# A two-layer hybrid encoder: the MLP's moving operand laid out in one run, the query norm of one attention group applied inside the exponential, attention weights normalised on VectorE

## The chip, the cores and the metric

The kernel runs on one core of one Trainium2 chip. The metric is the device time of one execution in microseconds. Engines are named as in the profile: PE is TensorE's matrix products (PEld its weight loads), DVE is VectorE, ACT is ScalarE, POOL is GpSimd, SP is SyncE, which here issues most of the DMAs.

## The reference

Two layers act on 256 tokens of width 2048, all in float32. Each layer normalises `x`, projects it once, and feeds three groups of attention heads from that one projection; the group outputs are normalised, concatenated and projected back. Then comes a squared-ReLU MLP of width 8192.

```python
for l in range(DEPTH):
    h = rmsnorm(x, norm_mix[l])
    proj = jnp.einsum('bsd,de->bse', h, w_in[l])
    qa, ka, va, qb, kb, vb, qc, kc, vc = jnp.split(proj, IN_SPLITS, axis=-1)
    oa = window_attention(...)
    ob = neighborhood_attention(...)
    oc = axial_global_attention(...)
    mix = jnp.concatenate([rmsnorm(oa, out_gain_a[l]), rmsnorm(ob, out_gain_b[l]), rmsnorm(oc, out_gain_c[l])], axis=-1)
    x = x + jnp.einsum('bse,ed->bsd', mix, w_o[l])
    h = rmsnorm(x, norm_mlp[l])
    u = jax.nn.relu(jnp.einsum('bsd,df->bsf', h, w_up[l]))
    x = x + jnp.einsum('bsf,fd->bsd', u * u, w_down[l])
return rmsnorm(x, norm_final)
```

The group that the change touches most is C, 16 query heads on 4 key heads of 64 columns:

```python
q = axial_rope(rmsnorm(q, q_gain), ang_row, ang_col)
k = axial_rope(rmsnorm(k, k_gain), ang_row, ang_col)
s = jnp.einsum('bqgrd,bkgd->bgrqk', q_blk, k).astype(jnp.float32) * scale
p = jax.nn.softmax(s, axis=-1).astype(v.dtype)
return jnp.einsum('bgrqk,bkgd->bqgrd', p, v)
```

The norm of a query is one number for each token and head, and the rotation is linear. So that number may be applied to the scores instead of the query.

## The kernel before

**Numbers as high and low parts.** Each operand of a product is split into a part rounded for TensorE (`fp32r`) and the rest. A product is then three products: high by high, high by low, low by high.

**Weights.** All weights are streamed in `steps` of 512 KB, 348 to a layer. `load` fetches a step, `split` makes its high part on ACT (L790) and its low part on DVE (L791, `wlo`), two steps ahead of its use. Input projection, output projection and the MLP's second product go through `mode_b` (L441): the activations are the stationary operand, and the weights' 512 columns move (L448 to L450).

**The MLP's first product** (`up_steps`, L613 and L615) is the other way round: a 128-column block of weights is stationary, and the normalised activations `ht` move. `ht` is a tile of `(2, 2, 256)`: part (high, low), block `kk` of 128 features, 256 tokens. L613 multiplies the high weights by both parts at once, so its 512 moving columns for one `kk` are two runs of 256 with another run between them. L615 multiplies the low weights by the high part only. `hprep` (L178) makes these tiles, for the MLP and for the input projection, which takes its stationary operand out of the same layout.

**Attention.** Work of the attention is cut into units of four (head, query block) pairs, 16 to a layer. A unit has three pieces. `unit_scores` (L317) makes the scores on PE, the negated row maximum on DVE, the exponential on ACT with that maximum as its bias and the row sum as a by-product (L345); then DVE takes the reciprocal of the sum (L353), and POOL multiplies the four blocks of weights by it (L355). `unit_transp` (L357) transposes the weights on PE and splits them (ACT L365, DVE L366). `unit_pv` (L368) multiplies by the values (L376, L383) and adds the two halves on DVE (L391, L396). When a pair of units is done, `mix_prep` (L400) prepares the output projection's operand and sums the squares on POOL (L410 to L419).

**The rotary chain** (`rope`, L278) serves group C's keys and queries. DVE squares and sums the raw rows (L283, L285); POOL takes mean and epsilon (L287), the power -1/2 (L235), multiplies the rows by it (L290) and then does the rotation: per block of 128 tokens a product with the cosine table (L296), four with the sine table (L300), and their sum (L508 for the queries, L495 for the keys). The second table's product is written over the tile of the squares. Queries come in two chunks a layer, `qc0` and `qc1`; they leave the projection through ACT (L503), and PE transposes them after the chain (`q_transposes`, L245).

**What sets the order.** Instructions of an engine run in program order. A hand-written planner, `tick` (L160), runs after each weight step and emits waiting pieces, when what they come after was emitted at least a given delay ago, counted in planned microseconds. The delays stand in one line, L49: `D_T` is from a unit's scores to its transposes, `D_RQ` from a chunk of queries to its transposes. In each layer the input projection's eight chunks run in the order of `IN_CHUNKS`, and the attention pieces are slipped between their steps and those of the output projection.

Of the kernel before, what the change touches and what calls it, by code (L numbers as in the profile page):

```python
# [43 lines left out]
def tile_trunk(ctx: ExitStack, tc: tile.TileContext, x_in, w_in, w_o, w_up, w_down,  # L44
# [4 lines left out]
    D_X, D_S, D_SS, D_T, D_PV, D_QK, D_RQ, D_RK, D_SQ = 6.0, 6.0, 7.0, 18.0, 6.0, 6.0, 24.0, 16.0, 6.0  # L49
# [14 lines left out]
    def big(dt, *shape):  # L64
        return dp.tile([P, *shape], dt, tag="big", bufs=24, name=nm("big"))
# [110 lines left out]


    def hprep(key, gcol, j, hT, ss, done, fin_rs, late=0):  # L178
# [99 lines left out]
    def rope(raw, H, which, l, outs):  # L278
# [8 lines left out]
        nc.gpsimd.tensor_scalar(ms, s, 1.0 / 64, EPS, op0=ALU.mult, op1=ALU.add)  # L287
        r = rsqrt(ms, n)
        rv = raw.rearrange("p t h d -> p (t h) d")
        nc.gpsimd.tensor_mul(rv, rv, r.rearrange("p (a o) -> p a o", o=1).to_broadcast([P, n, 64]))  # L290
        t1 = big(F32, NT, H, 64)
        ct, st = ctab[which, l], stab[which, l]
        t2 = sq.rearrange("p (t h d) -> p t h d", t=NT, h=H)
        for t in range(NT):
# [6 lines left out]
            outs(t, t1[:, t, :, :], t2[:, t, :, :])  # L301

# [14 lines left out]
    def unit_scores(u):  # L317
# [11 lines left out]
        if u.kind == "C":  # L329
            for b in range(2):  # L330
                nc.vector.tensor_reduce(negm[:, 2 * b:2 * b + 2], S[b], axis=AX.X, op=ALU.max, negate=True)
            src = [S[s // 2][:, s % 2, :] for s in range(4)]
# [11 lines left out]
        for s in range(4):  # L344
            nc.scalar.activation(p[:, s, :], src[s], AF.Exp, bias=negm[:, s:s + 1],  # L345
                                 accum_out=sums[:, s:s + 1])
# [7 lines left out]
        for s in range(4):  # L354
            nc.gpsimd.tensor_scalar(p[:, s, :], p[:, s, :], rs[:, s:s + 1], 1.0, op0=ALU.mult, op1=ALU.mult)  # L355
# [98 lines left out]
    def layer_steps(l):  # L454
# [12 lines left out]
        def proj_evac(name, banks):  # L467
# [32 lines left out]
            elif name in ("qc0", "qc1"):  # L500
# [8 lines left out]
                rope(raw, 8, "q", l, outs)  # L509
                i = int(name[2])  # L510
                kh, kl = st["k"]["C"]
                for g in range(2):
                    qT = big(F32R, 4, 256)
                    pq = add(lambda g=g, qT=qT: q_transposes(qs, 2 * g, qT), 0.45, delay=D_RQ)
                    for qb in range(2):
                        queue_unit(g_unit(l, st, "C", 2 * i + g, qb, qT, kh, kl, st["V"]["C"]), pq, st["kC"])
# [23 lines left out]
        for name in IN_CHUNKS:  # L540
# [5 lines left out]
            for k in range(nst):  # L546
# [47 lines left out]
        def up_steps(g):  # L594
            for c in range(2):
                fc = 2 * g + c
                box = {}
                for k in range(8):
# [3 lines left out]
                    def mm(wh, wl, k=k, fc=fc, box=box):  # L602
# [3 lines left out]
                        for kk in range(2):  # L606
                            for fs in range(4):
# [5 lines left out]
                                nc.tensor.matmul(o.rearrange("p (s c) -> p s c", s=2), sh, ht[:, :, kk, :],  # L613
                                                 start=s0, stop=False, skip_group_check=True)
                                nc.tensor.matmul(o[:, 0:256], sl, ht[:, 0, kk, :],  # L615
# [105 lines left out]
    def g_unit(l, st, kind, kv, qb, qT, kh, kl, V, bias=None):  # L721
        u = Unit()
        u.kind, u.l, u.kv, u.qb, u.qT, u.kh, u.kl, u.V = kind, l, kv, qb, qT, kh, kl, V
# [226 lines left out]
```

## Time and profile before

| | us |
|---|---|
| median of 3 runs | 2076.85 (2076.42 to 2078.95) |
| the profiled execution | 2079.79 |
| its span, first to last instruction | 2078.0 |

The profile is that of one execution. It gives, for each engine, when each instruction began and how long it took, and infers from semaphores what a waiting instruction waited for. Starts are counted from the first instruction. In a timeline row stand the start and the duration in us, the engine, the line, the operation, what it writes and reads, and in brackets the idle time of the engine before it with what ended it. In a row of a group stand the busy time in us and the mean ns of one, then the idle time. A row of a window gives the stretch, its length, the busy time and instruction count of PE, PEld, DVE, ACT and POOL, the granted clock of TensorE, the busy share of the DMA engines, and GB/s. The first layer's attention lies between about 70 and 310 us of the span, the second's at about 1100 to 1340; the MLPs fill the rest.

### The profile page before, as it was taken

To read this page: it belongs to the slowest core of one execution; us is meant where nothing else is said; L and a number is where in the kernel's file an instruction comes from. 1 tells how busy PE (TensorE), PEld (TensorE's weight loads), DVE (VectorE), ACT (ScalarE), POOL (GpSimd) and SP (SyncE) were. 2 spreads that over 40 slices of the span, in tenths; PEclk is the share of its full clock that TensorE was granted. 3 is DMA by queue.
4 is the path that set the end of the run, shared out by engine and by line. 5 is a ranking of instruction groups with operands and counts; after the bars stand their busy time and mean duration, and the time that the engine had idled before them with its cause. 6 is when DMAs were issued, how large, how long until landed. Compare 5 with 4: busy or idle time off the path is not lost.

```text
span 2078.0 us, 27361 instructions
## 1 busy us (share of the span) xinstructions
PE 2054.5 (99%) x10396; PEld 1736.4 (84%) x10396; DVE 1359.5 (65%) x1634; ACT 1045.0 (50%) x1536; POOL 274.6 (13%) x298
## 2 busy tenths in 40 slices
PE   8999999999999999999999999999999999999998
PEld 7878788888888888888888787888888888888886
DVE  6878976565565555656668789766565556656565
ACT  6657656444344443444556666555344444434444
POOL 0485420000000000000005843200000000000001
PEclk9999999999999999999999999999999999999999
DMA  8654465566666666666656454556656666665663
GB/s 287 182 156 151 152 192 178 186 192 184 194 189 191 188 188 193 187 189 191 187 179 189 142 159 123 193 173 190 192 187 192 190 186 193 190 191 187 191 212 122
DMA packets 107536, 381.25 MB, mean 183 GB/s; under 512 B 11875, under 2 KB 14691, under 8 KB 107404
## 3 DMA queue, kind: packets, MB, share of 16 engines
q1 hardware_dynamic: 107116, 378.45, 58.1%
q8 instruction: 81, 1.33, 0.3%
q10 hardware_dynamic: 288, 1.05, 0.1%
q14 instruction: 51, 0.42, 0.1%
HBM read 377.34 MB, written 2.11 MB: 183 GB/s over the span
## 4 chain that ended last, share of the span: by engine, by line
PE 93%; DVE 3%; POOL 2%; issue 1%; ACT 0%; DMA 0%; SPq 0%; POOLq 0%; DVEq 0%
PE mm L613 23%; PE mm L449 18%; PE mm L448 18%; PE mm L450 18%; PE mm L615 12%; PE tr L364 1%; PE tr L192 1%; DVE wlo L791 1%; PE mm L323 1%; PE mm L324 1%; DVE big L267 1%; POOL big L300 1%; PE tr L383 0%; POOL big L508 0%; POOL sm L235 0%
## 5 line engine op out<-in xcount | busy, mean ns | idle before, releaser
L791 DVE TENSOR_TENSOR wlo<-wraw,whi 128x1024 fp32r<-128x1024 f32 (+1 forms) x697 | 868.5, 1248 | 655.4 <-ACT whi L790 652.9
L790 ACT CAST whi<-wraw 128x1024 fp32r<-128x1024 f32 (+1 forms) x697 | 731.3, 1051 | 914.4 <-PE mm L450 477.3
L613 PE MATMUL mm<-big,whi 128*128 128x512 f32 x2048 | 724.4, 399 | 0.0
L448 PE MATMUL mm<-whi,big 128*128 128x512 f32 (+1 forms) x1792 | 696.2, 389 | 1.0 <-DVE x L585 1.0
L449 PE MATMUL mm<-wlo,big 128*128 128x512 f32 (+1 forms) x1792 | 693.2, 387 | 0.6 <-DVE wlo L791 0.4
L450 PE MATMUL mm<-whi,big 128*128 128x512 f32 (+1 forms) x1792 | 692.4, 386 | 0.0
L615 PE MATMUL mm<-big,wlo 128*128 128x256 f32 x2048 | 575.1, 281 | 0.0
L613 PEld LDWEIGHTS mm<-big,whi 128*128 128x128 f32 x2048 | 384.8, 188 | 95.8
L450 PEld LDWEIGHTS mm<-whi,big 128*128 128x128 f32 x1792 | 337.2, 188 | 68.6
L448 PEld LDWEIGHTS mm<-whi,big 128*128 128x128 f32 x1792 | 337.5, 189 | 67.5 <-DVE x L585 2.2
L449 PEld LDWEIGHTS mm<-wlo,big 128*128 128x128 f32 x1792 | 337.8, 189 | 66.6 <-DVE wlo L791 2.3
L615 PEld LDWEIGHTS mm<-big,wlo 128*128 128x128 f32 x2048 | 386.8, 189 | 0.5
L235 POOL TENSOR_TENSOR sm<-sm,mhalf 128x2 f32<-128x2 f32 (+3 forms) x16 | 23.7, 1482 | 785.0 <-DVE sm L230 770.9
L355 POOL TENSOR_SCALAR big<-big,sm 128x256 f32<-128x256 f32 x128 | 96.0, 767 | 224.7 <-DVE sm L353 200.0
L691 POOL TENSOR_TENSOR x<-x,big 128x512 f32<-128x512 f32 x6 | 8.6, 1456 | 722.6 <-ACT mid L695 722.6
L650 DVE SCALAR_TENSOR_TENSOR x<-mm,sm,x 128x512 f32<-128x512 f32 x128 | 89.9, 743 | 4.5 <-PE mm L450 4.5
L623 ACT COPY mid<-mm 128x256 f32<-128x256 f32 x128 | 46.6, 373 | 26.7 <-PE mm L615 26.7
L624 DVE TENSOR_TENSOR mid<-mid,mm 128x256 f32<-128x256 f32 x128 | 49.4, 419 | 0.0
L625 DVE SCALAR_TENSOR_TENSOR mid<-mid 128x512 f32<-128x512 f32 x64 | 44.0, 688 | 1.1
L629 DVE TENSOR_TENSOR big<-mid,big 128x512 fp32r<-128x512 f32 x64 | 43.8, 684 | 0.0
L366 DVE TENSOR_TENSOR big<-tr,big 128x512 fp32r<-128x512 f32 x64 | 41.1, 680 | 0.8 <-ACT big L365 0.5
L628 ACT CAST big<-mid 128x512 fp32r<-128x512 f32 x64 | 40.1, 626 | 2.8 <-DVE mid L625 0.2
(116 smaller groups left out, 1004.0 us busy)
## 6 DMA issues: line engine op xcount, KB each, us to landing
wraw<-in_w_up_dram SPq DMA_DIRECT2D x256, 512.0 KB, 3.5
wraw<-in_w_down_dram SPq DMA_DIRECT2D x256, 512.0 KB, 3.5
wraw<-in_w_in_dram SPq DMA_DIRECT2D x120, 512.0 KB, 3.6
wraw<-in_w_o_dram SPq DMA_DIRECT2D x64, 512.0 KB, 4.1
biasB<-in_rpb_dram SPq DMA_DIRECT2D x16, 349.5 KB, 5.6
biasA<-avec SPq DMA_DIRECT2D x4, 768.0 KB, 5.7
x<-in_x_dram SPq DMA_DIRECT2D x3, 512.0 KB, 9.5
big<-in_gfin_dram SPq DMA_DIRECT2D x2, 512.0 KB, 4.7
```

What stands on the lines that cost most here:

```text
L355: nc.gpsimd.tensor_scalar(p[:, s, :], p[:, s, :], rs[:, s:s + 1], 1.0, op0=ALU.mult, op1=ALU.mult)
L448: nc.tensor.matmul(o, a_h, wh[:, i, :], start=first and i == 0, stop=False)
L449: nc.tensor.matmul(o, a_h, wl[:, i, :], start=False, stop=False)
L450: nc.tensor.matmul(o, a_l, wh[:, i, :], start=False, stop=last and i == len(sub) - 1)
L613: nc.tensor.matmul(o.rearrange("p (s c) -> p s c", s=2), sh, ht[:, :, kk, :], start=s0, stop=False, skip_group_check=True)
L615: nc.tensor.matmul(o[:, 0:256], sl, ht[:, 0, kk, :], start=False, stop=s1, skip_group_check=True)
L623: nc.scalar.copy(ai, o[:, 256:512])
L624: nc.vector.tensor_add(ai, ai, o[:, 0:256])
L625: nc.vector.scalar_tensor_tensor(a, a, 0.0, a, op0=ALU.max, op1=ALU.mult)
L650: nc.vector.scalar_tensor_tensor(xs, box["b"][t], st["r2"][:, t:t + 1], xs, op0=ALU.mult, op1=ALU.add)
L790: last_hi[0] = nc.scalar.copy(h[:, part], w[:, part]).ins
L791: nc.vector.tensor_sub(lo[:, part], w[:, part], f(h[:, part]))
```

## The change

There are three edits, and two planned delays that go with them.

1. `hprep` makes its tiles as `(2, 512)`: block `kk`, then both parts side by side, 256 columns each. A helper, `halves`, shows such a tile in the old order of axes to everything else that uses it. In `up_steps` both moving operands are now one run.
2. For the queries of group C, `rope` rotates the raw rows. Mean, epsilon and power are done on POOL behind the rotation and kept in a tile `rq`. The row maximum is multiplied by `rq` on DVE, and the exponential takes `rq` as its scale. The keys keep the old way. The second table's product gets a tile of its own, `t2`.
3. The four products of the weights with the reciprocal of the sum move from POOL to DVE.

`D_T` goes from 18 to 15 and `D_RQ` from 24 to 20.

```diff
-    D_X, D_S, D_SS, D_T, D_PV, D_QK, D_RQ, D_RK, D_SQ = 6.0, 6.0, 7.0, 18.0, 6.0, 6.0, 24.0, 16.0, 6.0
+    D_X, D_S, D_SS, D_T, D_PV, D_QK, D_RQ, D_RK, D_SQ = 6.0, 6.0, 7.0, 15.0, 6.0, 6.0, 20.0, 16.0, 6.0
...
+    def halves(rows):
+
+        return rows.rearrange("p k (s c) -> p s k c", s=2)
...
-            hh = big(F32R, 2, 2, 256)
-            hT[2 * j + h] = hh
+            rows = big(F32R, 2, 512)
+            hT[2 * j + h] = rows
+            hh = halves(rows)
...
-        nc.gpsimd.tensor_scalar(ms, s, 1.0 / 64, EPS, op0=ALU.mult, op1=ALU.add)
-        r = rsqrt(ms, n)
-        rv = raw.rearrange("p t h d -> p (t h) d")
-        nc.gpsimd.tensor_mul(rv, rv, r.rearrange("p (a o) -> p a o", o=1).to_broadcast([P, n, 64]))
+        if which == "k":
+            nc.gpsimd.tensor_scalar(ms, s, 1.0 / 64, EPS, op0=ALU.mult, op1=ALU.add)
+            r = rsqrt(ms, n)
+            rv = raw.rearrange("p t h d -> p (t h) d")
+            nc.gpsimd.tensor_mul(rv, rv, r.rearrange("p (a o) -> p a o", o=1).to_broadcast([P, n, 64]))
         t1 = big(F32, NT, H, 64)
+        t2 = big(F32, NT, H, 64)
         ct, st = ctab[which, l], stab[which, l]
-        t2 = sq.rearrange("p (t h d) -> p t h d", t=NT, h=H)
...
+        if which == "k":
+            return
+        nc.gpsimd.tensor_scalar(ms, s, 1.0 / 64, EPS, op0=ALU.mult, op1=ALU.add)
+        r = sp.tile([P, n], F32, tag="rq", bufs=3, name=nm("rq"))
+        nc.gpsimd.tensor_tensor(r, ms, mhalf[:, 0:n], op=ALU.pow)
+        return r
...
+            nc.vector.tensor_mul(negm, negm, u.rq)
...
             nc.scalar.activation(p[:, s, :], src[s], AF.Exp, bias=negm[:, s:s + 1],
+                                 scale=u.rq[:, s:s + 1] if u.kind == "C" else 1.0,
                                  accum_out=sums[:, s:s + 1])
...
-            nc.gpsimd.tensor_scalar(p[:, s, :], p[:, s, :], rs[:, s:s + 1], 1.0, op0=ALU.mult, op1=ALU.mult)
+            nc.vector.tensor_scalar(p[:, s, :], p[:, s, :], rs[:, s:s + 1], None, op0=ALU.mult)
...
-                    hts = [st["hT"][(k * nk + i) // 2] for i in range(nk)]
+                    hts = [halves(st["hT"][(k * nk + i) // 2]) for i in range(nk)]
...
-                                nc.tensor.matmul(o.rearrange("p (s c) -> p s c", s=2), sh, ht[:, :, kk, :],
-                                                 start=s0, stop=False, skip_group_check=True)
-                                nc.tensor.matmul(o[:, 0:256], sl, ht[:, 0, kk, :],
+                                nc.tensor.matmul(o, sh, ht[:, kk, :], start=s0, stop=False, skip_group_check=True)
+                                nc.tensor.matmul(o[:, 0:256], sl, ht[:, kk, 0:256],
```

**Where instructions move: POOL at the first layer's first chunk of queries.** These are POOL's rows before, from the weights' normalisation (L355) of three units to the end of the queries' rotary chain.

```order
L355 TENSOR_SCALAR big_808<-big_808,sm_824 128x256 x4
L355 TENSOR_SCALAR big_896<-big_896,sm_912 128x256 x4
L355 TENSOR_SCALAR big_1011<-big_1011,sm_1027 128x256 x4
L287 TENSOR_SCALAR sm_1103<-sm_1101 128x16
L235 TENSOR_TENSOR sm_1105<-sm_1103,mhalf 128x16
L290 TENSOR_TENSOR big_1095<-big_1095,sm_1105 128x1024
L296 TENSOR_TENSOR big_1108<-big_1095,ctab_q_443 128x512
L300 TENSOR_TENSOR big_1099<-big_1095,stab_q_444 128x8x16 x4
L296 TENSOR_TENSOR big_1108<-big_1095,ctab_q_443 128x512
L508 TENSOR_TENSOR big_1098<-big_1108,big_1099 128x512
L300 TENSOR_TENSOR big_1099<-big_1095,stab_q_444 128x8x16 x4
L508 TENSOR_TENSOR big_1098<-big_1108,big_1099 128x512
```

And these are POOL's rows at the same place now, where L424 and L429 are the old L410 and L415, L302, L306 and L522 the old L296, L300 and L508, and `rq` is the tile that the exponential's scale comes from.

```order
L424 TENSOR_TENSOR mid_1092<-mid_978 128x512
L429 TENSOR_TENSOR sqacc_1094<-mid_1092 128x256
L302 TENSOR_TENSOR big_1123<-big_1114,ctab_q_443 128x512
L306 TENSOR_TENSOR big_1124<-big_1114,stab_q_444 128x8x16 x4
L302 TENSOR_TENSOR big_1123<-big_1114,ctab_q_443 128x512
L522 TENSOR_TENSOR big_1117<-big_1123,big_1124 128x512
L306 TENSOR_TENSOR big_1124<-big_1114,stab_q_444 128x8x16 x4
L522 TENSOR_TENSOR big_1117<-big_1123,big_1124 128x512
L310 TENSOR_SCALAR sm_1122<-sm_1120 128x16
L312 TENSOR_TENSOR rq_1138<-sm_1122,mhalf 128x16
```

The units' products and the queries' norm stood ahead of the rotation; now the squares of the mix stand there, and mean and power stand behind it. On PE the transposes of these queries stand twelve rows, one weight step, earlier.

**Where instructions move: DVE in the first layer's output projection.** These are DVE's rows before, from the low part of one weight step (`wlo`) on; the lines between belong to units of group B (L342, L353, L396) and to the residual (L585).

```order
L791 TENSOR_TENSOR wlo_2523<-wraw_2286,whi_2522 128x1024
L342 TENSOR_REDUCE sm_2505<-big_2504 128x4
L585 SCALAR_TENSOR_TENSOR x<-mm_2464,sm_1418,x 128x512
L585 SCALAR_TENSOR_TENSOR x<-mm_2465,sm_1418,x 128x512
L791 TENSOR_TENSOR wlo_2543<-wraw_2346,whi_2542 128x1024
L353 RECIPROCAL sm_2514<-sm_2506 128x4
L396 TENSOR_TENSOR mid_2455<-tr_2560,ot_2565 64x2x128 x2
L791 TENSOR_TENSOR wlo_2581<-wraw_2408,whi_2580 128x1024
```

And these are DVE's rows now from the low part of the same weight step on (L807 is the old L791, L355 the old L342, L601 the old L585, L367 the old L353, L443 the old L429, L405 the old L391, L380 the old L366; L369 is the product that came from POOL).

```order
L807 TENSOR_TENSOR wlo_2592<-wraw_2355,whi_2591 128x1024
L355 TENSOR_REDUCE sm_2574<-big_2573 128x4
L601 SCALAR_TENSOR_TENSOR x<-mm_2533,sm_1399,x 128x512
L601 SCALAR_TENSOR_TENSOR x<-mm_2534,sm_1399,x 128x512
L807 TENSOR_TENSOR wlo_2619<-wraw_2407,whi_2618 128x1024
L367 RECIPROCAL sm_2583<-sm_2575 128x4
L443 TENSOR_SCALAR sm_2612<-tr_2609 128x2
L369 TENSOR_SCALAR big_2573<-big_2573,sm_2583 128x256 x4
L405 TENSOR_TENSOR mid_2647<-tr_2636,ot_2645 64x256 x2
L380 TENSOR_TENSOR big_2651<-tr_2652,big_2650 128x512
L380 TENSOR_TENSOR big_2651<-tr_2659,big_2650 128x512
L807 TENSOR_TENSOR wlo_2669<-wraw_2469,whi_2668 128x1024
```

Between two weight splits DVE now has the four products of a unit, and the pieces of the units stand earlier, so that more of them come before a given split. Over the seven weight steps from the low part that before is `wlo_2431` to the one that is `wlo_2702`, there are 16 such products now, and none before.

More of the change, by code (lines that the diff above doesn't have):

```diff
@@ L508, in outs @@
                     nc.gpsimd.tensor_add(qs[:, t, :].rearrange("p (h d) -> p h d", h=8), a, b)
-                rope(raw, 8, "q", l, outs)
+                rq = rope(raw, 8, "q", l, outs)
                 i = int(name[2])
@@ L515, in proj_evac @@
                     for qb in range(2):
-                        queue_unit(g_unit(l, st, "C", 2 * i + g, qb, qT, kh, kl, st["V"]["C"]), pq, st["kC"])
+                        c0 = qb * 8 + 4 * g
+                        queue_unit(g_unit(l, st, "C", 2 * i + g, qb, qT, kh, kl, st["V"]["C"],
+                                          rq=rq[:, c0:c0 + 4]), pq, st["kC"])
             elif name == "qa":
@@ L719, in bias_a, with g_unit @@
         return tb
-    def g_unit(l, st, kind, kv, qb, qT, kh, kl, V, bias=None):
+    def g_unit(l, st, kind, kv, qb, qT, kh, kl, V, bias=None, rq=None):
         u = Unit()
+        u.rq = rq
         u.kind, u.l, u.kv, u.qb, u.qT, u.kh, u.kl, u.V = kind, l, kv, qb, qT, kh, kl, V
```

## The prediction

> **What bounds the kernel now.** I read the page's busy times first, then the chain of work that ended last, then TensorE's (PE's) start times.
>
> ```profile
> PE 2054.5 (99%) x10396; PEld 1736.4 (84%) x10396; DVE 1359.5 (65%) x1634; ACT 1045.0 (50%) x1536; POOL 274.6 (13%) x298
> PE 93%; DVE 3%; POOL 2%; issue 1%; ACT 0%; DMA 0%; SPq 0%; POOLq 0%; DVEq 0%
> L613 PE MATMUL mm<-big,whi 128*128 128x512 f32 x2048 | 724.4, 399 | 0.0
> ```
>
> The chain is 93% PE, so an edit counts if it shortens the step from one matmul to the next, or removes a place where PE stands still. Durations of matmuls overlap (a start every 0.23 us, each 0.39 us long); only start times tell the cost. Three streams of starts:
>
> ```profile
> 549.12 0.39 PE L448 MATMUL mm<-whi,big 128*128 128x512 f32 x1
> ...
> 551.16 0.39 PE L448 MATMUL mm<-whi,big 128*128 128x512 f32 x1
> ...
> 39.82 0.28 PE L450 MATMUL mm<-whi,big 128*128 128x256 f32 x1
> ...
> 41.02 0.28 PE L448 MATMUL mm<-whi,big 128*128 128x256 f32 x1
> ...
> 560.25 0.40 PE L613 MATMUL mm<-big,whi 128*128 128x512 f32 x1
> 560.49 0.28 PE L615 MATMUL mm<-big,wlo 128*128 128x256 f32 x1
> ...
> 561.31 0.40 PE L613 MATMUL mm<-big,whi 128*128 128x512 f32 x1
> ```
>
> Nine 512-column products of one run take 2.04 us, 226.7 ns each. Ten 256-column products take 1.20 us, 120 ns each. The first product of the MLP alternates L613 (512 columns in two runs of 256) with L615 (256): three pairs take 1.06 us, 353.3 ns a pair. The two streams would give 226.7 + 120 = 346.7.
>
> **Edit 1, one run.** The pair costs 6.6 ns more than its two parts do elsewhere, and the only difference I see is the break between the runs. Rounded to the streams' common step (226.7 = 34 x 6.67, 120 = 18 x 6.67, 353.3 = 53 x 6.67) it is one step of 6.67 ns. There are 2048 pairs: 2048 x 6.67 = **13.65 us** saved. Bounds: nothing; and two steps, 27.3 us, for which the first pair after a stream of 512s speaks:
>
> ```profile
> 553.20 0.39 PE L613 MATMUL mm<-big,whi 128*128 128x512 f32 x1
> ...
> 553.54 0.40 PE L613 MATMUL mm<-big,whi 128*128 128x512 f32 x1
> ```
>
> That pair took 0.34 us with its break, once; the next ones take 353. I take one step, since the steady streams give it and 340 is seen only on entering. L613's row has no idle time of PE before it, and the engines that split its weights are busy 65% and 50% of the span, so they can follow a faster PE.
>
> **Edit 2, the norm of C's queries.** The rotary chain on GpSimd (POOL) now ends too late once a layer:
>
> ```profile
> PE tr L245 <- POOL big L508: 5.5, 2, 2.8
> 104.18 3.87 POOL L355 TENSOR_SCALAR big<-big,sm 128x256 f32<-128x256 f32 x4 [10.88 <-DVE sm L353]
> 108.13 1.05 POOL L287 TENSOR_SCALAR sm<-sm 128x16 f32<-128x16 f32 x1
> 109.26 3.76 POOL L235 TENSOR_TENSOR sm<-sm,mhalf 128x16 f32<-128x16 f32 x1
> 113.10 2.15 POOL L290 TENSOR_TENSOR big<-big,sm 128x1024 f32<-128x1024 f32 x1
> 115.33 1.35 POOL L296 TENSOR_TENSOR big<-big,ctab_q 128x512 f32<-128x512 f32 x1
> ...
> 125.77 2.12 POOL L508 TENSOR_TENSOR big<-big,big 128x512 f32<-128x512 f32 x1
> 102.96 1.24 ACT L503 ACTIVATE big<-mm,sm 128x512 f32<-128x512 f32 x2
> 124.89 0.27 PE L245 MATMUL tr<-ident,big 128*128 128x128 f32 x1
> 127.94 0.99 PE L245 MATMUL tr<-ident,big 128*128 128x128 f32 x7 [2.78 <-POOL big L508]
> 128.68 0.48 PE L448 MATMUL mm<-whi,big 128*128 128x512 f32 x1
> ...
> 132.64 0.39 PE L449 MATMUL mm<-wlo,big 128*128 128x512 f32 x1
> 120.00:133.00 13.00, 10.22 (x43) 8.14 (x42) 10.01 (x12) 6.61 (x10) 12.17 (x12) 0.87 0.53 164
> ```
>
> PE's second transpose starts at 127.94 instead of 0.11 after 124.89 (the last seven take 0.74): 2.94 us lost. Then the granted clock is down (0.87 over the window), and ten matmuls from 128.68 to 132.64 take 3.96 us instead of 2.27: 1.69 more. That is 4.63 a layer, **9.3 us** for two.
>
> The raw queries are there at 104.20 (L503's end). POOL is then held by the weights' normalisation (3.87), and by L287, L235 and L290 (to 115.33); all of it leaves the front of the chain. From the first L296 to the last L508 it is 12.56 us. In the changed order, POOL has the mix's L410 and L415 ahead of the chain. They need a VectorE (DVE) result of about the same time, so I start the chain between 104.2 and 108, and it ends between 116.8 and 120.6. PE reaches these transposes twelve rows, one step of 12 x 226.7 = 2.72 us, sooner: 122.2. So there is 1.6 to 5.4 us of room and the wait goes. At the bad end it stays as it is, and nothing is gained.
>
> The mean square and the power stand behind the rope now. Their 1.05 + 3.76 end by 121.6 to 125.4. The new wait is DVE's product of the row maximum with `rq`; DVE's weight splits queue behind it. That unit's scores come only after transposes at 122.2, their copies and a planned delay, so it doesn't bind. It adds 16 products of four columns, 0.26 us each by L351's row (below), in 140 to 200, where DVE is busy 45.81 of 60: free. The scale operand may cost ScalarE up to 32 ns on each of 64 exponentials (a scaled copy, L406, against L345, below), 2 us beside the 41.06 of 60 that it is busy: nothing on PE's path.
>
> **Edit 3, weights normalised on DVE.** 128 pieces leave POOL, which has no time to lose, for an engine that binds in two stretches a layer:
>
> ```profile
> L355 POOL TENSOR_SCALAR big<-big,sm 128x256 f32<-128x256 f32 x128 | 96.0, 767 | 224.7 <-DVE sm L353 200.0 <-DVE sm L429 13.7 <-ACT big L503 10.9
> L707 DVE TENSOR_SCALAR x<-x,sm 128x1024 f32<-128x1024 f32 x2 | 1.5, 754 | 1.3 <-POOL sm L235 1.3
> L353 DVE RECIPROCAL sm<-sm 128x4 f32<-128x4 f32 x32 | 5.5, 172 | 9.8 <-ACT big L345 9.5
> L351 DVE TENSOR_TENSOR sm<-sm,sm 128x4 f32<-128x4 f32 x8 | 2.1, 258 | 3.6 <-ACT sm L350 3.4
> L345 ACT ACTIVATE big<-mm,sm 128x256 f32<-128x256 f32 x64 | 29.5, 472 | 23.3 <-DVE sm L331 22.8
> L406 ACT ACTIVATE big<-mid,gn 128x256 fp32r<-128x256 f32 x32 | 15.0, 504 | 18.5 <-DVE mid L396 6.6 <-POOL big L753 6.5 <-DVE mid L391 3.4
> 92.00:113.00 21.00, 20.70 (x103) 16.96 (x102) 19.52 (x28) 15.38 (x29) 9.95 (x7) 1.00 0.59 173
> 223.28:262.23 38.95, 37.33 (x193) 30.26 (x191) 38.40 (x53) 27.55 (x55) 14.78 (x18) 1.00 0.43 139
> 110.18 0.41 DVE L396 TENSOR_TENSOR mid<-tr,ot 64x256 f32<-64x256 f32 x1
> 110.51 1.27 DVE L366 TENSOR_TENSOR big<-tr,big 128x512 fp32r<-128x512 f32 x2
> 111.24 1.09 PE L383 MATMUL tr<-big,mid 128*128 128x512 f32 x3 [0.30 <-DVE big L366]
> 261.00 1.23 DVE L791 TENSOR_TENSOR wlo<-wraw,whi 128x1024 fp32r<-128x1024 f32 x1
> ...
> 264.75 0.40 PE L449 MATMUL mm<-wlo,big 128*128 128x512 f32 x1
> 140.00:200.00 60.00, 60.00 (x310) 50.99 (x309) 45.81 (x60) 41.06 (x92) 39.04 (x45) 1.00 0.53 166
> ```
>
> The price of a piece is not in the trace. L707 is this very operation with 1024 columns (754 ns), and L353 has 4 (172). On the line between them, 256 columns cost 172 + 252 x 0.571 = 316 ns; I take **0.31 us** as an estimate from those rows. Bounds: 0.172 below, and 0.767 above, what POOL pays (L707's whole duration is about that).
>
> In 92 to 113, DVE is busy 19.52 of 21.00, and PE already waits for L366. Three units bring 12 x 0.31 = 3.7; 1.5 of idle time takes part of it; 2.2 reach PE. In 223 to 262, DVE is busy 38.40 of 38.95. The order puts 16 pieces ahead of the weight split that began at 261.00, and other work that changes places there is worth 0.8 (two more L366, 1.27; two more L353, 0.34; four L396 fewer and two more L391 of that size, -0.82). PE used that split at 264.75, 2.5 after its end. So 16 x 0.31 + 0.8 - 2.5 = 3.3 reach PE. Together 5.5 a layer, **11.0 us** of new stalls; 3.2 with the low price, 36.6 with the high one. The other units fall where DVE has the idle time just shown.
>
> **Sum.** -13.65 - 9.3 + 11.0 = -11.95 us. The profiled execution took 2079.79 us, so 2067.8. That execution lies 2.94 above the median of 2076.85 shown; in terms of the median: **2064.9 us**, -0.58%.
>
> **Rivals.** *The break costs nothing* (the 6.67 ns belongs to alternating long and short products): edits 2 and 3 remain, -9.3 + 11.0, 2078.5. For it: the first pair ran at 0.34 with its break. The Trainium skill (Advanced Engine Details and Errata, SBUF Cachelines) counts the cost of a read by 16-byte lines, and asks for two hits on a line; runs of 256 fp32 fill their lines either way, so by that rule the break is free. Against it: the two steady streams add up to one step less.
>
> *Two steps*: the short product also drops to 113, the pair to 340: 2051.2. For it that same entering pair; against it 120 ns in every steady 256 stream.
>
> *The query wait stays*, because L410's input comes late from a DVE that is now slower in just that stretch: 2074.2.
>
> *DVE becomes the bound*, the case that ends slower. POOL still runs ropes, squares and bias sums in both stretches (9.95 and 14.78 us busy above), and DVE pieces that collide with them take what POOL's did, 0.767: 12 x 0.767 - 1.5 + 16 x 0.767 + 0.8 - 2.5 = 18.3 a layer, 36.6 in all, and 2076.85 - 22.95 + 36.6 = 2090.5. It decides from 28 p - 3.2 = 11.5, a piece of p = 0.52 us.
>
> ```profile
> L355 POOL TENSOR_SCALAR big<-big,sm x128: 470/478/2511, 71.3 to 1303.0; 128x256 f32<-128x256 f32 x128
> ```
>
> The Trainium skill (SBUF — State Buffer, Who interferes with whom) says that a DVE operation in a two-port mode and GpSimd exclude each other for a whole instruction; the spread of POOL's pieces beside a busy DVE (470 to 2511, mean 767) goes that way, but no row has a DVE operation of that kind beside POOL. Against this rival: POOL itself loses 96 us of work, so there is less to collide with.
>
> **Chances.** Forecast 0.53 (its own range 2057 to 2073, from the low price to some of the query wait left), break free 0.12, two steps 0.15, query wait stays 0.07, DVE binds 0.13. A measurement of this kernel can tell about 0.2% from no change, 2072.7 to 2081.0. So faster 0.68 (forecast and two steps), same 0.19 (break free, query wait), slower 0.13. The range takes in all but the last, with the low price beside two steps: 2048 to 2080.
>
> **What would show it.** Edit 1: three pairs of the MLP's first product in 1.04 us (1.06: no gain; 1.02: two steps). Edit 2: PE's row of waits for L508's successor gone, and full clock in 120 to 133. Edit 3: the mean of the new DVE pieces near 310 ns, and PE's waits for L366, L396 and the weight split longer by some 5 us a layer; above 0.52 us a piece I am wrong on the sign.

## The result: slower by 1.2%, and the profile after

| | before | after |
|---|---|---|
| median of 4 runs, us | 2077.86 | 2103.68 (2102.69 to 2104.84) |
| span of the profiled execution, us | 2078.0 | 2102.6 |
| mean granted clock of TensorE | 0.998 | 0.992 |

The ratio is 1.0124, 95% interval 1.0111 to 1.0137. The forecast of 2064.9 has the wrong sign. Line numbers have moved: L613 and L615 are now L629 and L630; L448 to L450 are L462 to L464; L791 is L807; the scaling by the reciprocal, L355, is L369; the exponential L345 is L358; the weights' transposes L364 are L378 and their low half L366 is L380; the product with V, L383, is L397; L396 is L410, L407 is L421, L283 and L285 are L288 and L290, the queries' transposes L245 are L250.

First rows of the page after: busy times, the chain that ended last, and two groups (busy us and mean ns, then idle time before them); the third group is from the view by lines.

```profile
PE 2062.0 (98%) x10396; PEld 1742.7 (83%) x10396; DVE 1398.3 (67%) x1778; ACT 1049.4 (50%) x1536; POOL 176.6 (8%) x166
PE 88%; DVE 9%; issue 1%; ACT 1%; DMA 0%; SPq 0%; DVEq 0%; POOLq 0%; POOL 0%; ACTq 0%
L629 PE MATMUL mm<-big,whi 128*128 128x512 f32 x2048 | 724.4, 399 | 0.0
L369 DVE TENSOR_SCALAR big<-big,sm 128x256 f32<-128x256 f32 x128 | 48.4, 440 | 0.8
L250 PE MATMUL tr<-ident,big 128*128 128x128 f32 x64 | 8.9, 274 | 0.0
```

DVE's share of the chain went from 3% to 9%, while its busy time rose by only 39 us. The MLP's long product has the same 724.4 us as before. The queries' transposes (last row) wait for nothing now. In their place stand other waits; these are PE's, grouped by what it waited for (us in total, times, longest):

```profile
PE tr L397 <- DVE big L380: 15.4, 4, 5.6
PE tr L378 <- ACT big L358: 3.7, 2, 1.9
...
PE mm L463 <- DVE wlo L807: 2.4, 6, 0.7
```

The longest is at the first layer's third unit, and again in the second layer. PE's rows there, then DVE's, then POOL's (start, duration, in brackets idle time and what ended it):

```profile
98.36 1.07 PE L397 MATMUL tr<-big,mid 128*128 128x512 f32 x4
...
101.99 1.03 PE L378 MATMUL tr<-ident,big 128*128 128x128 f32 x8
...
111.04 0.39 PE L397 MATMUL tr<-big,mid 128*128 128x512 f32 x1
117.00 1.65 PE L397 MATMUL tr<-big,mid 128*128 128x512 f32 x3 [5.57 <-DVE big L380]
```

```profile
102.18 0.68 DVE L272 TENSOR_TENSOR big<-tr,big 64x512 fp32r<-64x512 f32 x1
...
103.08 1.40 DVE L272 TENSOR_TENSOR big<-tr,big 64x512 fp32r<-64x512 f32 x2
104.52 0.42 DVE L410 TENSOR_TENSOR mid<-tr,ot 64x256 f32<-64x256 f32 x1
...
105.57 1.20 DVE L807 TENSOR_TENSOR wlo<-wraw,whi 128x1024 fp32r<-128x1024 f32 x1
106.68 3.73 DVE L369 TENSOR_SCALAR big<-big,sm 128x256 f32<-128x256 f32 x4
110.34 1.28 DVE L421 SCALAR_TENSOR_TENSOR big<-mid,gn,big 128x256 fp32r<-128x256 f32 x2
111.55 1.47 DVE L288 TENSOR_TENSOR big<-big 128x1024 f32<-128x1024 f32 x1
112.94 2.28 DVE L807 TENSOR_TENSOR wlo<-wraw,whi 128x1024 fp32r<-128x1024 f32 x1
115.14 1.21 DVE L290 TENSOR_REDUCE sm<-big 128x16 f32<-128x1024 f32 x1
116.27 1.27 DVE L380 TENSOR_TENSOR big<-tr,big 128x512 fp32r<-128x512 f32 x2
```

```profile
105.59 2.07 POOL L424 TENSOR_TENSOR mid<-mid 128x512 f32<-128x512 f32 x1 [17.78 <-DVE mid L410]
...
108.44 1.34 POOL L302 TENSOR_TENSOR big<-big,ctab_q 128x512 f32<-128x512 f32 x1
109.75 2.19 POOL L306 TENSOR_TENSOR big<-big,stab_q 128x128 f32<-128x128 f32 x4
```

PE transposed this unit's weights at 101.99, and DVE wrote their low half only at 116.27. DVE was not idle: it was that far behind, with the next unit's four scalings (3.73 us), the other units' mix (L410, L421), the last of the keys' low parts (L272), the query chunk's squares and sums (L288, L290) and two weight splits (L807) ahead of the low half. PE reached the product with V at 111.04, and stood 5.6 us. The next view, of windows (length, busy us and count of PE, PEld, DVE, ACT, POOL, granted clock, DMA share, GB/s), shows what that cost besides:

```profile
101.90:117.50 15.60, 10.03 (x48) 8.14 (x47) 15.40 (x23) 9.29 (x19) 11.83 (x12) 0.90 0.38 111
114.38:121.21 6.83, 4.21 (x14) 3.62 (x15) 6.79 (x9) 1.75 (x3) 6.75 (x6) 0.50 0.45 130
120.00:133.00 13.00, 13.00 (x61) 10.86 (x60) 8.00 (x12) 5.33 (x8) 5.15 (x4) 0.95 0.65 206
```

DVE is busy 15.40 of 15.60 us while PE is busy 10.03; from 114.38 on the clock is at half for 6.83 us, and its end, at 121.21, is what takes the last row below full clock. In the first of these windows DVE was as full before, and PE hardly idle:

```profile
101.90:117.50 15.60, 15.30 (x75) 12.30 (x75) 15.27 (x19) 11.57 (x20) 13.00 (x10) 1.00 0.71 222
```

So a full DVE does not by itself stop PE; what differs is what stands ahead of the low half when PE asks for it. Lost PE time can be counted as follows: for every matmul, take the step to the next one less the median step of its line and shape, and add up what lies over 20 ns. This gives 54.9 us after and 30.8 before. The 24.1 between them account for nearly all of the 24.6 by which the span grew.

### The profile page after: what moved, and what is told of

It is laid out like the page before. It is cut to its first block, busy times and chain, and to the rows that moved or that the text cites. A ratio compares the mean times of both kernels' runs of the same rounds, so it can differ in the third digit from the quotient of the medians.

```text
span 2102.6 us, 27351 instructions
## 1 busy us (share of the span) xinstructions
PE 2062.0 (98%) x10396; PEld 1742.7 (83%) x10396; DVE 1398.3 (67%) x1778; ACT 1049.4 (50%) x1536; POOL 176.6 (8%) x166
## 4 chain that ended last, share of the span: by engine, by line
PE 88%; DVE 9%; issue 1%; ACT 1%; DMA 0%; SPq 0%; DVEq 0%; POOLq 0%; POOL 0%; ACTq 0%
PE mm L629 23%; PE mm L463 17%; PE mm L464 17%; PE mm L462 17%; PE mm L630 12%; DVE wlo L807 2%; DVE big L369 1%; DVE big L380 1%; ACT big L358 1%; DVE big L272 1%; PE tr L378 1%; PE tr L196 1%; DVE big L421 1%; PE tr L397 1%; DVE big L348 1%
## 5 line engine op out<-in xcount | busy, mean ns | idle before, releaser
L807 DVE TENSOR_TENSOR wlo<-wraw,whi 128x1024 fp32r<-128x1024 f32 (+1 forms) x697 | 862.3, 1239 | 642.5 <-ACT whi L806 640.3
L629 PE MATMUL mm<-big,whi 128*128 128x512 f32 x2048 | 724.4, 399 | 0.0
L462 PE MATMUL mm<-whi,big 128*128 128x512 f32 (+1 forms) x1792 | 697.6, 391 | 4.0 <-DVE big L257 1.7
L464 PE MATMUL mm<-whi,big 128*128 128x512 f32 (+1 forms) x1792 | 694.1, 387 | 0.0
L630 PE MATMUL mm<-big,wlo 128*128 128x256 f32 x2048 | 576.1, 281 | 0.0
L629 PEld LDWEIGHTS mm<-big,whi 128*128 128x128 f32 x2048 | 385.4, 188 | 95.0
L462 PEld LDWEIGHTS mm<-whi,big 128*128 128x128 f32 x1792 | 338.4, 189 | 71.3 <-issue 2.5
L464 PEld LDWEIGHTS mm<-whi,big 128*128 128x128 f32 x1792 | 338.5, 189 | 68.4
L630 PEld LDWEIGHTS mm<-big,wlo 128*128 128x128 f32 x2048 | 387.8, 189 | 0.5
L240 POOL TENSOR_TENSOR sm<-sm,mhalf 128x2 f32<-128x2 f32 (+2 forms) x12 | 12.8, 1067 | 812.9 <-DVE sm L235 782.4
L358 ACT ACTIVATE big<-mm,sm,rq 128x256 f32<-128x256 f32 x64 | 35.3, 561 | 31.2 <-DVE sm L344 31.1
L369 DVE TENSOR_SCALAR big<-big,sm 128x256 f32<-128x256 f32 x128 | 48.4, 440 | 0.8
L424 POOL TENSOR_TENSOR mid<-mid 128x512 f32<-128x512 f32 x16 | 27.1, 1692 | 255.8 <-DVE mid L410 197.1
```

What stands on the lines that cost most here:

```text
L369: nc.vector.tensor_scalar(p[:, s, :], p[:, s, :], rs[:, s:s + 1], None, op0=ALU.mult)
L462: nc.tensor.matmul(o, a_h, wh[:, i, :], start=first and i == 0, stop=False)
L464: nc.tensor.matmul(o, a_l, wh[:, i, :], start=False, stop=last and i == len(sub) - 1)
L629: nc.tensor.matmul(o, sh, ht[:, kk, :], start=s0, stop=False, skip_group_check=True)
L630: nc.tensor.matmul(o[:, 0:256], sl, ht[:, kk, 0:256], start=False, stop=s1, skip_group_check=True)
L807: nc.vector.tensor_sub(lo[:, part], w[:, part], f(h[:, part]))
```

## The experiments

All are timed beside the kernel before, whose medians lay at 2077.05 to 2077.83 in the four sets.

### The edits one at a time

**One run** (edit 1 alone): the kernel before, with `rows = big(F32R, 2, 512)` and both moving operands in one run.

> The kernel before with edit 1 alone (the MLP's moving operand in one run). Theory A (the break between two runs of 256 columns is free): the pair of L613 and L615 stays at 353.3 ns, as in the changed kernel's profile, and the time within 0.1% of before. Theory B (the break costs 6.67 ns, hidden in the changed kernel by something else): 346.7 ns a pair and 13.65 us less.

2078.97 us, ratio 1.0005 (0.9996 to 1.0015). A long and a short product still take 353.3 ns together. The saving of 13.65 us is excluded; in this stream the break between the runs is free. In the changed kernel too, three pairs last 575.50 - 574.43 = 1.07 us:

```profile
574.43 0.40 PE L629 MATMUL mm<-big,whi 128*128 128x512 f32 x1
574.67 0.28 PE L630 MATMUL mm<-big,wlo 128*128 128x256 f32 x1
...
575.50 0.40 PE L629 MATMUL mm<-big,whi 128*128 128x512 f32 x1
```

**Norm in the exponential** (edit 2 alone, with its delay):

```diff
-D_T, ..., D_RQ = 18.0, ..., 24.0
+D_T, ..., D_RQ = 18.0, ..., 20.0
```

> The kernel before with edit 2 alone (norm of C's queries inside the exponential, D_RQ 20; POOL still normalises the weights, D_T 18). If the loss comes from DVE's new pieces alone: the wait of the queries' transposes goes, no half-clock spell behind it, about 9 us less than before. If rotating first also costs (the mix's squares ahead of the chain, the wait for rq): no gain, or up to 5 us more than before.

2072.69 us, ratio 0.9975 (0.9965 to 0.9984): 4.8 us faster. The window that had a granted clock of 0.87 before has full clock:

```profile
120.00:133.00 13.00, 12.90 (x67) 10.57 (x66) 12.24 (x14) 8.63 (x13) 12.18 (x9) 1.00 0.55 165
PE mm L458 <- DVE wlo L803: 3.4, 4, 1.0
```

The wait is gone, and with PE earlier others appear: the second row (of PE's waits) is the weight split, for which PE waited 0.4 us in all before. The gain is about half of the 9 us expected; the part on the prediction comes back to it.

**Weights on DVE** (edit 3 alone, with `D_T` 15; the query norm stays on POOL with `D_RQ` 24):

> The kernel before with edit 3 alone (weights normalised on DVE, D_T 15). If DVE's new pieces are the loss: the queries' wait stays (9 us, in before as well), and new stalls of about 30 us come, so 2100 to 2110. If the loss needs edits 2 and 3 together (POOL's rope begins earlier and meets DVE's pieces): under 2090.

2102.19 us, ratio 1.0118 (1.0103 to 1.0133), so edit 3 with its delay is enough for the whole loss. The places are others than in the whole change: the waits of the queries' transposes for POOL grow from 5.5 to 10.6 us, and the product with V waits 4.9, not 15.4.

**Grouped**: the kernel before, with the MLP's first product in another order, four long products ahead of four short ones; still two runs.

```diff
+for low in range(2):
     for fs in range(4):
...
```

> The kernel before with the MLP's first product in another order: four high products of a feature block, then the four low ones, instead of one high and one low by turns; the same products, the operand still in two runs. If alternating long and short products costs the 6.67 ns: eight products take 4 x 226.7 + 4 x 120 = 1386.8 ns instead of 1413.2, and 2048 pairs 13.5 us less. If the two runs cost them: 1413 ns, no change. If a short product after a short one is what costs 120 (113 after a long one): longer, up to 1440 ns and 13.6 us more.

2072.86 us, ratio 0.998 (0.9971 to 0.9989). In the timeline (x4: four products in one row) four pairs take 593.74 - 592.34 = 1.40 us; the mean is 350.8 ns a pair, and long follows long in 233.6.

```profile
592.34 1.09 PE L611 MATMUL mm<-big,whi 128*128 128x512 f32 x4
593.27 0.64 PE L614 MATMUL mm<-big,wlo 128*128 128x256 f32 x4
593.74 1.09 PE L611 MATMUL mm<-big,whi 128*128 128x512 f32 x4
```

### Edit 3 taken apart: the pieces, their form, the delay

At this point the theory was the pieces themselves: they run beside POOL. By the trace after, 88 of the 128 hardly touch a POOL instruction and take 348 ns on average; the other 40 lie beside POOL, most of them wholly, and take 643 on average (the 667 in an expectation below is not borne out); the longest takes 1380. The rival was the delay of the weights' transposes, which edit 3 cut from 18 to 15.

**After, on POOL**: the changed kernel with one line undone, delay 15.

```diff
-            nc.vector.tensor_scalar(p[:, s, :], p[:, s, :], rs[:, s:s + 1], None, op0=ALU.mult)
+            nc.gpsimd.tensor_scalar(p[:, s, :], p[:, s, :], rs[:, s:s + 1], 1.0, op0=ALU.mult, op1=ALU.mult)
```

> The first two edits with the shorter delay of the weights' transposes (D_T 15), the weights normalised on GpSimd as before. If the 128 pieces on VectorE make the changed kernel slow, this one stays near the run of the second edit alone, 2072.7 us (2069 to 2077), and PE's waits at the product with V shrink to under 1 us each. If the shorter delay does it (PE reaches the weights three rows sooner, before they are normalised), it stays above 2085.

2082.26 us, ratio 1.0022 (1.0013 to 1.0032), between the two. The second edit gave 2072.69 with a delay of 18 (and two runs in the MLP, which by the first run makes no difference); 15 costs 9.6 us with no piece on DVE.

**Pieces out**: the changed kernel without L368 and L369, delay 15; it leaves out the normalisation of the weights.

> The changed kernel without the 128 pieces; it leaves out the normalisation of the attention weights. If the pieces are the whole cost of the third edit: 2068 to 2075 us, and the wait of 5.7 us at the product with V is gone. If a third or more of the cost lies elsewhere (the delay of 15, the order on VectorE): 2080 or more, with waits of over 2 us at the product with V left.

2082.38 us, ratio 1.0022 (1.0013 to 1.0032). Even with no normalisation anywhere the delay's cost is there, and its largest waits are again at the product with V (L395 here):

```profile
PE tr L395 <- DVE big L378: 8.9, 4, 2.3
```

**One product a unit**: the same scaling as one DVE instruction over 1024 columns.

```diff
-        for s in range(4):
-            nc.vector.tensor_scalar(p[:, s, :], p[:, s, :], rs[:, s:s + 1], None, op0=ALU.mult)
+        nc.vector.tensor_tensor(p, p, rs.rearrange("p (a o) -> p a o", o=1).to_broadcast([P, 4, 256]), op=ALU.mult)
```

> The changed kernel with one VectorE product per unit (128 x 1024, the reciprocals spread over the columns) in place of four scalings with a scalar per row. If the cost is the collision of that form of scaling with GpSimd (348 ns a piece alone, 667 beside GpSimd, 1380 at most), the product takes about the same 1.1 to 1.5 us whether GpSimd works or not, the four-piece group of 3.73 us at 106.7 becomes 1.5 or less, and the time falls to 2078 to 2092 us. If it is the plain load on VectorE's queue (1.1 to 1.4 us a unit in either form), the time stays within 5 us of 2103.7.

2103.18 us, ratio 1.0112 (1.0094 to 1.0130): the same as with four pieces, though a unit now costs DVE 1424 ns instead of 4 x 440, and none took over 2064 where a group of pieces took 3.73 us.

```profile
L368 DVE TENSOR_TENSOR big<-big,sm x32: 1206/1226/2064, 71.0 to 1318.2; 128x1024 f32<-128x1024 f32 x32
```

The waits lie elsewhere (the weight split 8.4 us, POOL's sum of squares 6.9, the product with V only 4.3) and come to the same. The collision with POOL is seen in both forms (18 of the products stay clear of POOL and take 1223 ns, 14 lie beside it and take 1682), but its extent doesn't set the time.

**The changed kernel with a delay of 18**: one number differs.

```diff
-D_T = 15.0
+D_T = 18.0
```

> The changed kernel with the weights' transposes delayed by 18 as before, not 15. With GpSimd normalising, 15 for 18 cost 2082.3 - 2072.7 = 9.6 us. If the delay and the pieces cost separately, this gives 2103.7 - 9.6 = 2094 (2091 to 2097), so the pieces cost 21 at either delay. If the pieces hurt only because the delay was cut under them, it comes near 2075 to 2085. If VectorE is full in these stretches whatever the delay, it stays above 2099.

2079.92 us, ratio 1.0010 (1.0001 to 1.0020): 23.8 us come back with one planned number. The expectation that the two costs add (2094) was wrong; it is the case in which the delay was cut under the pieces. The same stretch, PE's rows, then DVE's, then the window:

```profile
102.78 1.03 PE L378 MATMUL tr<-ident,big 128*128 128x128 f32 x8
...
106.39 1.07 PE L397 MATMUL tr<-big,mid 128*128 128x512 f32 x4
...
110.01 1.07 PE L397 MATMUL tr<-big,mid 128*128 128x512 f32 x4
```

```profile
92.53 2.80 DVE L272 TENSOR_TENSOR big<-tr,big 64x512 fp32r<-64x512 f32 x4 [0.70 <-ACT big L270]
...
103.48 2.22 DVE L288 TENSOR_TENSOR big<-big 128x1024 f32<-128x1024 f32 x1
105.63 1.97 DVE L369 TENSOR_SCALAR big<-big,sm 128x256 f32<-128x256 f32 x4
107.52 1.21 DVE L290 TENSOR_REDUCE sm<-big 128x16 f32<-128x1024 f32 x1
108.64 1.27 DVE L380 TENSOR_TENSOR big<-tr,big 128x512 fp32r<-128x512 f32 x2
...
111.01 0.84 DVE L410 TENSOR_TENSOR mid<-tr,ot 64x256 f32<-64x256 f32 x2
...
113.25 2.10 DVE L421 SCALAR_TENSOR_TENSOR big<-mid,gn,big 128x256 fp32r<-128x256 f32 x2
```

```profile
101.90:117.50 15.60, 15.60 (x78) 12.94 (x77) 15.51 (x22) 9.68 (x15) 14.94 (x14) 1.00 0.50 152
```

The transposes start within 0.8 us of where they did, but the low half follows after 5.9 us instead of 14.3, and the product with V runs through at 110.01. With 15 the pair of units ahead was multiplied with V at 98.36, here at 106.39 (the pair's second product); so with 15 its mix (L410, L421) stood in DVE's queue ahead of this unit's low half, and POOL's squares (L424) fell beside this unit's neighbour's scalings. With 18 the same L410 comes at 111.01 and L421 at 113.25, behind it. L272, the keys' low parts, was done at 95.3. Of the 8.4 us between 14.3 and 5.9, weight splits that now come first are some 2.8, the mix is 2.1, L272 another 2.1, and the slower scalings are 1.8; the query chunk's squares give 0.7 back. DVE is as full as with 15 (15.51 of 15.60), and PE does not stop.

**A delay of 24:**

> The changed kernel with a delay of 24. If the pieces are a matter of latency (the weights come later by the pieces' time, and PE has to ask later), a longer delay covers them: 2070 to 2082. If VectorE's queue is simply longer than PE's work in these stretches, PE waits for the weight splits instead and the time stays within 4 us of the kernel with 18.

2107.36 us, ratio 1.0135 (1.0120 to 1.0150). Neither theory's number. The product with V is no longer the worst; the mix is now too late for the output projection, and PE waits once a layer for POOL's last sum of squares (first row; the second is the window of the half clock that goes with it):

```profile
145.84 1.11 PE L441 MATMUL tr<-ones,sqacc 128*128 128x64 f32 x4 [11.06 <-POOL sqacc L433]
139.34:149.57 10.23, 3.73 (x11) 3.15 (x12) 2.34 (x6) 0.00 (x0) 6.87 (x7) 0.50 0.21 72
```

**Grouped, in one run:**

> The order with four long products ahead of four short ones (2072.9 us with two runs), and the moving operand in one run. If the break between the runs costs a step of 6.67 ns once long products follow one another (233.6 there against 226.7 in the projections), it takes 226.7 ns and about 2072.9 - 768 x 2 x 6.67 / 1000 = 2062.6 us. If the break is free and it is the change of bank or the pattern that costs the step, 2072.9 within 2 us, 233.6 ns a step as before.

2072.37 us, ratio 0.9969 (0.9956 to 0.9982), 233.6 ns from long to long as with two runs. The break is free in this stream too. This run's trace also shows something of the clock. It has the same two waits of the queries' transposes as before (first row), and the clock stays full (second row; 0.87 before):

```profile
PE tr L251 <- POOL big L514: 5.6, 2, 2.8
120.00:133.00 13.00, 10.21 (x50) 8.30 (x49) 10.10 (x12) 7.55 (x12) 12.32 (x12) 1.00 0.52 164
```

**By banks**: the kernel before; for each of the four PSUM banks both blocks' long products, then both short ones; two runs.

```diff
+for fs in range(4):
+    for low in range(2):
+        for kk in range(2):
...
```

> Two runs; for each of the four banks both long products and then both short ones, so that long follows long in one bank, and the bank changes once in four products as against once in two before and at each one in the grouped order. If the change of bank costs the step: long to long 226.7, pair mean 348 to 350, 2067 to 2073 us. If the break costs it: long to long 233.6 as in the grouped order, and a time of 2073 to 2078.

2067.37 us, ratio 0.9944 (0.9930 to 0.9959): 9.7 faster. Two pairs take 697 ns on average, 348.5 a pair:

```profile
592.24 0.62 PE L611 MATMUL mm<-big,whi 128*128 128x512 f32 x2
592.71 0.40 PE L614 MATMUL mm<-big,wlo 128*128 128x256 f32 x2
592.94 0.63 PE L611 MATMUL mm<-big,whi 128*128 128x512 f32 x2
```

The time came out as the change of bank would have it, but not the steps: long to long stays at 233 ns within one bank, and against the grouped order it is the short ones that fell, from 118.5 to 115.3 on average. So the time depends on the order of the products; what the step belongs to stays open.

### What is left at 18, and a better version

**Pieces out, 18:**

> The changed kernel with a delay of 18 and without the 128 pieces; it leaves out the normalisation of the attention weights. TensorE's order is that of the run with 18 and pieces, 2079.9 us. If the pieces' load on VectorE is what is left of the third edit's cost there, this gives about 2072.7 (the second edit alone, GpSimd normalising; 2070 to 2075). If VectorE has room for the pieces at 18 and the 7.2 us come from elsewhere, 2078 or more.

2072.31 us, ratio 0.9975 (0.9965 to 0.9984). With POOL normalising it was 2072.69: at this delay POOL did that work at no cost in time.

**One product a unit, 18:**

> The changed kernel with a delay of 18 and one product a unit (1.23 us) in place of four scalings (1.14 alone, 1.6 as they ran in the run with 18: 398 ns a piece). If the scalings' slow runs beside GpSimd cost the 7.2 us there, 2072 to 2076. If it is the load, in either form: 2077 to 2083.

2080.05 us, ratio 1.0010 (1.0000 to 1.0019). The form doesn't matter here either; the 7.6 to 7.7 us over the run without pieces are the load.

**A delay of 20:**

> The changed kernel with a delay of 20. If the delay is cover that VectorE's queue needs, and 18 is enough of it, the waits at the product with V stay under 0.5 us each; the loss at 24 came at the mix's sum of squares (11.2 us a layer), which waits for the last units, and should grow with the delay past 18: 2080 to 2095. If 18 is a notch (a matter of which work falls before which), 20 may lie anywhere, above 2095 too, with waits at places that neither 15 nor 24 shows.

2088.87 us, ratio 1.0056 (1.0041 to 1.0071). Waits of up to 1.9 us for an exponential (191.50), 1.5 at the scores (238.68) and 1.5 at the product with V: the largest are not those of 15 or 24. Of the four delays tried, 18 is the only good one, which speaks for what falls before what rather than for enough cover.

**Edit 2 with the grouped order, and with the order by banks** (POOL normalising, delay 18):

> The second edit with its delay of 20, and the MLP's first product with its four long products ahead of its four short ones; the weights normalised on GpSimd, two runs in the moving operand. If the two gains lie in different places they add: 2077.5 - 4.8 - 4.6 = 2068 us (2066 to 2070). If they share a cover, 2071 to 2073.

> The second edit with its delay of 20, GpSimd normalising with 18, and the MLP's first product bank by bank (both long products of a bank, then both short ones). The two gains lie in different places and add: 2077.1 - 4.8 - 9.7 = 2062.6 us (2060 to 2065).

2067.56 (ratio 0.9947, 0.9933 to 0.9962) and 2061.75 us (0.9924, 0.9909 to 0.9939). The gains add to within 1.6 us, and the last is below both kernels.

## Why the prediction was wrong, step by step

The runs on place and delay in one table, in us; all with edit 2 (POOL's run at 18 has two runs of columns in the MLP, the others one, which makes no difference):

| weights normalised by | D_T 15 | 18 | 20 | 24 |
|---|---|---|---|---|
| POOL | 2082.26 | 2072.69 | | |
| nobody | 2082.38 | 2072.31 | | |
| DVE, four scalings | 2103.68 (the change) | 2079.92 | 2088.87 | 2107.36 |
| DVE, one product | 2103.18 | 2080.05 | | |

**Edit 1, -13.65 predicted: nothing.** The step that failed is "the only difference I see is the break between the runs". There was another, the alternation itself, which the first rival named, and the runs with another order gain 4.6 and 9.7 us with the break left in. The Trainium skill's rule on 16-byte lines (Advanced Engine Details and Errata, SBUF Cachelines), by which runs of 256 columns cost nothing, is borne out: 353.3 ns a pair with one run and with two.

**Edit 2, -9.3 predicted: -4.8.** The mechanism was right: wait and half clock at those transposes are gone, alone and in the whole change. The size was off in two ways. The lost PE time, counted as above, fell by only 7.4 us (30.8 to 23.4), since 1.9 of new waits appeared, at the weight split above all, as PE came earlier. And the profiled execution of before, from which the 9.3 was read, lay 2.3 us above the median of the runs beside which edit 2 was timed. The clock's 1.69 a layer was charged to every execution, and the traces don't bear that out: the two waits of 2.8 us stand in five traces (before, one run, grouped, grouped in one run, by banks), and of the ten only six come with a spell at half clock. That this is why the profiled execution took longer than the median is likely and not shown. One more estimate was too small: the scale operand cost ScalarE 89 ns an exponential (561 against 472), not up to 32, but in the run of edit 2 alone PE has no wait for an exponential over 0.3 us. In the changed kernel the gain is used up: with edits 1 and 2 it takes 2103.7, without them 2102.2.

**Edit 3, +11.0 predicted: +31 (2103.68 - 2072.69).** Two terms were wrong, in different directions.

- The price of a piece, 0.31 us, was nearly right for a piece alone (0.348). It was 0.440 on average, because of POOL. Yet at the old delay, with 0.398 us a piece, they cost 7.2 us; the prediction's own sum would give (28 x 0.398 - 3.2) x 2 = 15.9. Counting pieces in two stretches overcharged: at the weight splits, to which it gave 3.3 a layer, PE waits 0.4 at 18 and 1.2 at 15 (2.4 for both layers, in the waits above).
- The delay had no term at all. The prediction took PE's times of asking from before and only made DVE later: "together 5.5 a layer" of new stalls at the waits that were there. This is the step that fails. `D_T` moves PE's requests, and with them the order of DVE's queue. Cut by 3 planned us, it costs 9.6 us where POOL normalises, and 23.8 where DVE does, whose queue is longer by the pieces. For 92 to 113 the prediction had 2.2 a layer; at the product with V that waited 0.30 before (at 111.24) PE now waits 5.57 (117.00), because the unit's low half stands behind work that came earlier for the same reason. And PE waits where the prediction had nothing ("The other units fall where DVE has the idle time just shown"), for an exponential and at a later product with V:

```profile
169.14 0.66 PE L378 MATMUL tr<-ident,big 128*128 128x128 f32 x4 [1.87 <-ACT big L358]
213.49 0.80 PE L397 MATMUL tr<-big,big 128*128 128x512 f32 x1 [2.13 <-DVE big L380]
```

Along the runs, from before to edit 2, to the pieces on DVE at 18, to the delay of 15, the steps are -4.8, +7.2 and +23.8. They add up to the whole change because each begins where the last one ended; the sum is no check of the account.

**The rivals.** "The break costs nothing" was true. "DVE becomes the bound" had the sign, and both together give 2090.5 + 13.65 = 2104.2, the measured time; but that is partly chance. Its price of 0.767 us a piece was not reached, and the collision from which it took that price isn't what decides: a form that suffers less of it gives the same time at both delays. Pieces beside POOL take 643 ns on average against 348 alone, but the twelve that lie beside nothing but POOL's power (L240, L312) take 341 to 384. The Trainium skill (SBUF — State Buffer, Who interferes with whom) has a DVE operation in a two-port mode and GpSimd exclude each other for a whole instruction; the first of these numbers goes that way, the second shows that not every POOL instruction holds a piece up. What decides, as far as the runs show, is what stands ahead on DVE when PE asks.

That delay and pieces together make the loss is shown by the table. How they make it was seen in the timelines at the largest wait, and not tried by itself (the order of DVE alone, with PE's kept). With one product a unit, and with edit 3 alone, about the same loss comes at other waits, so no single wait is the cause.

## What to carry to other kernels

A planner's delay is a term of its own: when a change moves one, list for every consumer when it asks before and after, and what then stands ahead in the producer's queue. Idle time of an engine counts only in the stretch where the work lands, and the busy share does not tell whether anyone waits: in the same 15.6 us DVE was busy 15.27 before and 15.40 after, and PE 15.30 and 10.03. Work moved to a full engine is paid for by what it stands ahead of, as well as by its duration. A step of a few nanoseconds between two streams is no proof of the one difference that comes to mind; try the order of the instructions as well as their layout.

## What the runs showed of the hardware

- Spells at half clock come in pieces of one length: 6.83 us with PE's stand of 5.6 us, 10.24 with that of 11.06, and 3.41 at each wait for the queries in the trace before: two, three and one times 3.41. The Trainium skill (TensorE: Matmul & The Clock Gate, Part 1) gives a window of 3413 ns, and this trace agrees. In the attention, four spells hold 20.5 us after the change, in 4.4 of which PE stands waiting, and two hold 6.8 before, with 0.2 of waiting. Half of the difference of what is left is an estimate of what the clock itself cost: some 4.8 of the 24.1 us of lost PE time.
- The same wait of 2.8 us came with a half-clock spell in six of ten cases (both layers before and in the grouped order, one of two layers with one run and by banks, neither in the grouped order in one run). So one profile gives the wait, but not the clock's share of a typical execution.
- The same 4096 products of the MLP, with the same operands, take 353.3, 350.8 or 348.5 ns a pair by their order alone; by 2048 pairs these are 5 and 10 us, and the runs gained 4.6 and 9.7. In the grouped order the first four long products behind a stream of 512s follow each other in 227, the later ones in 233.
